# An RMSNorm with SiLU on one core: the root by GpSimd's power, squares moved to ScalarE, gamma in one piece, VectorE's instructions at an edge

## The chip, the core and the metric

The kernel runs on one core of a Trainium2 chip. The metric is device time in microseconds (us). Three runs before the change took 316.83, 316.88 and 316.90 us; their median is 316.88. One further execution was profiled. Its span, from the first to the last instruction, is 315.43 us.

## What is computed

```python
def reference(x, gamma, eps):
    rms = np.sqrt(np.mean(x ** 2, axis=-1, keepdims=True) + eps)
    out = gamma * x / rms
    return (out * (1 / (1 + np.exp(-out)))).astype(np.float32)
```

x has the shape 8 x 1024 x 2048 in float32, so 8192 rows of 2048 numbers; gamma has 2048 and eps is 1e-5. 67.1 MB are read and 67.1 MB written.

## The kernel before

The 8192 rows are cut into 16 blocks of 512. A block lies in SBUF as 128 partitions with J = 4 rows each, 32 KB a partition, 4.19 MB in all. A ring of BUFS = 6 such blocks (`xt`) holds the data; a block is loaded, worked on in place and stored from the same place. So load b + 6 has to wait until store b has landed. Blocks 4 and 5 are loaded by one transfer of twice the size (`load_pair`, L69).

Loads are issued from ScalarE's instruction stream (L67, L71), stores from SyncE's (L117). Each stream runs in its own order, so an instruction that waits holds what stands behind it. The order is written out by hand (`tc.manual_schedule`, L119).

A block b passes these steps:

- `squares_scalar(b)` (L73) and `squares_vector(b)` (L84): the sum of squares of each of its four rows. ScalarE does the first `share(b)` rows with Square and an accumulator (L78), VectorE the others with a multiply-and-reduce (L86). Each of these shows in the profile as two instructions, the operation and the reading of the accumulator. The results go to `ss`, 128 x 4. `share` is 2, but 1 for the even blocks from 4 to 12. The products themselves go to PSUM and are not used.
- `root(b)` (L93): ScalarE takes the square root of ss / d + eps (L95). In the trace a table load (ACT_TABLE_LOAD) precedes each change between Sqrt and Silu; Square has none of its own beside either.
- `invert(b)` (L98): VectorE's reciprocal of that, `rstd`, 128 x 4 (L100).
- `multiply(b)` (L103): VectorE multiplies each row by its rstd and by gamma, four instructions (L105), each with two tensors of SBUF as inputs.
- `silu(b)` (L108): ScalarE applies Silu to two rows at a time (L113), then SyncE issues the store. The argument `between` issues a load between the two halves.

The main loop (L145) does the squares and the root of block b + 1 together with the product and the Silu of block b: for the first three blocks and the last one the product comes first, for the others the squares. From block 8 on, the load of block b + 3 is issued within `squares_scalar(b + 1)`, behind its first square; loads 6 and 7 are issued at b = 3. The last block (L174) is done in another way: VectorE multiplies each row by gamma alone (L177) and ScalarE's Silu takes rstd as its scale, row by row (L179).

At the start gamma is loaded into one partition (L125), copied to all 128 by TensorE with a matrix of ones (L128) and brought from PSUM to `g` by VectorE (L130). A Square of one element (L124) warms ScalarE up. Lines 198 and 212 in the profile stand for the framework's instructions at the start and at the end.

The instructions of an engine are read from memory in blocks, by transfers of their own (queue q14 in the profile).

Of the kernel before, what the change touches and what calls it, by code (L numbers as in the profile page):

```python
# [1 line left out]

# [4 lines left out]

ACT = mybir.ActivationFunctionType
ALU = mybir.AluOpType


@with_exitstack
def kernel(
    ctx: ExitStack,
    tc: tile.TileContext,
    x: bass.AP,
    gamma: bass.AP,
    eps: bass.AP,
    out: bass.AP,
):  # L20

    nc = tc.nc
    P = nc.NUM_PARTITIONS
    f32 = mybir.dt.float32
    x2 = x.flatten_outer_dims()
    o2 = out.flatten_outer_dims()  # L30
    n, d = x2.shape
    J = 4
    BUFS = 6
    nblk = n // (P * J)
    PAIRS = (4,)

    def view(t, b):

        for q in PAIRS:
            if b in (q, q + 1):  # L40
                both = t[q * P * J:(q + 2) * P * J, :].rearrange("(p j) d -> p (j d)", p=P, j=2 * J)
                return both[:, (b - q) * J * d:(b - q + 1) * J * d]
        return t[b * P * J:(b + 1) * P * J, :].rearrange("(p j) d -> p (j d)", p=P, j=J)

    singles = ctx.enter_context(tc.tile_pool(name="singles", bufs=1))
    small = ctx.enter_context(tc.tile_pool(name="small", bufs=2))
    psum = ctx.enter_context(tc.tile_pool(name="psum", bufs=1, space=bass.MemoryType.PSUM))

    Q = 4
    w = d // Q  # L50
    g = singles.tile([P, d], f32)
    eps_t = singles.tile([P, 1], f32)
    ones = singles.tile([P, P], f32)
    junk_a = psum.tile([P, d], f32, name="junk_a")
    junk_v = psum.tile([P, d], f32, name="junk_v")
    ring = singles.tile([P, BUFS * J * d], f32, name="xt")
    sss, rmss, rstds = {}, {}, {}

    def rows(b, j, k):
        at = (b % BUFS) * J + j  # L60
        return ring[:, at * d:(at + k) * d]

    def row(b, j):
        return rows(b, j, 1)

    def load(b):
        nc.scalar.dma_start(out=rows(b, 0, J), in_=view(x2, b))  # L67

    def load_pair(b):  # L69
        both = x2[b * P * J:(b + 2) * P * J, :].rearrange("(p j) d -> p (j d)", p=P, j=2 * J)  # L70
        nc.scalar.dma_start(out=rows(b, 0, 2 * J), in_=both)  # L71

    def squares_scalar(b, loads=()):  # L73


        sss[b] = small.tile([P, J], f32, name="ss")
        for j in range(share(b)):
            nc.scalar.activation(out=junk_a, in_=row(b, j), func=ACT.Square,  # L78
                                 accum_out=sss[b][:, j:j + 1])
            if j == 0:  # L80
                for s in loads:
                    load(s)

    def squares_vector(b):  # L84
        for j in range(share(b), J):
            nc.vector.tensor_tensor_reduce(  # L86
                out=junk_v, in0=row(b, j), in1=row(b, j), scale=1.0, scalar=0.0,
                op0=ALU.mult, op1=ALU.add, accum_out=sss[b][:, j:j + 1])

    def share(b):  # L90
        return 1 if 4 <= b <= 12 and b % 2 == 0 else 2

    def root(b):  # L93
        rms = small.tile([P, J], f32, name="rms")
        nc.scalar.activation(out=rms, in_=sss.pop(b), func=ACT.Sqrt, scale=1.0 / d, bias=eps_t)  # L95
        rmss[b] = rms

    def invert(b):  # L98
        rstd = small.tile([P, J], f32, name="rstd")
        nc.vector.reciprocal(out=rstd, in_=rmss.pop(b))  # L100
        rstds[b] = rstd

    def multiply(b):  # L103
        for j in range(J):
            nc.vector.scalar_tensor_tensor(out=row(b, j), in0=row(b, j), scalar=rstds[b][:, j:j + 1],  # L105
                                           in1=g, op0=ALU.mult, op1=ALU.mult)

    def silu(b, between=()):  # L108
        for h in range(0, J, 2):
            if h:  # L110
                for s in between:
                    load(s)
            nc.scalar.activation(out=rows(b, h, 2), in_=rows(b, h, 2), func=ACT.Silu)  # L113
        store(b)

    def store(b):
        nc.sync.dma_start(out=view(o2, b), in_=rows(b, 0, J))  # L117

    with tc.manual_schedule():  # L119

        load(0)
        nc.vector.memset(ones, 1.0)  # L122
        nc.vector.memset(eps_t, float(eps))
        nc.scalar.activation(out=junk_a[:, 0:1], in_=ones[:, 0:1], func=ACT.Square)  # L124
        nc.sync.dma_start(out=g[0:1, :], in_=bass.AP(tensor=gamma.tensor, offset=gamma.offset, ap=[[d, 1], [1, d]]))  # L125
        for c in range(Q):
            cols = slice(c * w, (c + 1) * w)
            nc.tensor.matmul(junk_v[:, cols], ones[0:1, :], g[0:1, cols], start=True, stop=True)  # L128
        load(1)
        nc.vector.tensor_copy(out=g, in_=junk_v)  # L130
        nc.scalar.copy(out=junk_a[:, 0:1], in_=junk_v[:, d - 1:d])  # L131
        for b in range(2, PAIRS[0]):
            load(b)
        for b in PAIRS:
            load_pair(b)

        last = nblk - 1
        SOON = 3  # L140
        squares_scalar(0)
        squares_vector(0)
        root(0)
        invert(0)
        for b in range(last):  # L145
            loads = [b + 3] if BUFS + 2 <= b + 3 < nblk else []
            between = []
            if b + 3 == BUFS:

                load(BUFS)  # L150
                between = [BUFS + 1]
            if b < SOON:
                multiply(b)
                squares_scalar(b + 1, loads)
                silu(b)
                squares_vector(b + 1)
                root(b + 1)
            elif b < last - 1:
                squares_scalar(b + 1, loads)
                squares_vector(b + 1)  # L160
                root(b + 1)
                multiply(b)
                silu(b, between)
            else:
                multiply(b)
                squares_scalar(b + 1)
                silu(b)
                squares_vector(b + 1)
                root(b + 1)
            if b + 1 < last:  # L170
                invert(b + 1)


        for j in range(J):  # L174
            if j == J // 2:
                invert(last)
            nc.vector.tensor_mul(out=row(last, j), in0=row(last, j), in1=g)  # L177
        for j in range(J):
            nc.scalar.activation(out=row(last, j), in_=row(last, j), func=ACT.Silu,  # L179
                                 scale=rstds[last][:, j:j + 1])  # L180
        store(last)


# [1 line left out]
_INS = ['x', 'gamma', 'eps']  # L185
_OUTS = [((8, 1024, 2048), 'float32')]

_NUMBERS = {'eps': 9.999999747378752e-06}


# [26 lines left out]
```

## Time and profile before

| what | us |
|---|---|
| median of three runs | 316.88 |
| span of the profiled execution | 315.43 |
| VectorE (DVE) busy | 235.2 |
| ScalarE (ACT) busy | 212.5 |
| TensorE (PE) busy | 7.2 |
| GpSimd (POOL) busy | 0.2 |
| VectorE, 60 products (L105), 2.346 each | 137.0 |
| VectorE, 37 squares (L86), 2.296 each | 85.0 |
| ScalarE, 30 Silu of two rows (L113), 3.610 each | 107.3 |
| ScalarE, 27 squares (L78), 1.873 each | 50.6 |
| ScalarE, 31 table loads, 1.283 each | 39.8 |
| ScalarE, 16 square roots (L95), 0.297 each | 4.8 |
| first store issued, last store issued | 35.29, 291.55 |
| last store landed | 314.61 |

The table gives times of one execution, from the profiled one but for its first line. DMA stands for the 16 engines that move data between HBM and SBUF; all queues share them. A queue's transfer is made of packets; here most have 32 KB, one partition's four rows. The queue q10 holds the loads, q1 the stores and gamma. The profile's DMA line gives the busy share of the engines in tenths, in 40 equal slices of the span, and the packet records give the start, length, queue and size of each packet, without the engine that moved it. An idle time in the list of waits is put down to what ended it.

### The profile page before, as it was taken

Reading aid. Unit: us, or ns where it says so; the run is one execution under the profiler, and the core shown is the slowest. Engines: PE = TensorE matmul, PEld = TensorE weight load, DVE = VectorE, ACT = ScalarE, POOL = GpSimd, SP = SyncE. Lnnn points to the kernel's source line nnn. Section 1 sums busy time; section 2 is a strip of 40 time slices with the busy share of each in tenths; the row PEclk is TensorE's granted clock in tenths of the full one; section 3 lists DMA queues with packets and bytes.
Section 4 is the critical chain, followed back from the end, with each engine's and each line's share of the span. In section 5 each row is a group of like instructions: output and inputs, shape, how many; then the busy total and the mean of one; then the engine's idle time right before and its main releaser. Section 6 shows DMA issues by size and latency. Waiting matters only on the chain.

```text
span 315.4 us, 436 instructions
## 1 busy us (share of the span) xinstructions
PE 7.2 (2%) x8; PEld 2.5 (1%) x8; DVE 235.2 (75%) x157; ACT 212.5 (67%) x137; POOL 0.2 (0%) x4
## 2 busy tenths in 40 slices
PE   6300000000000000000000000000000000000000
PEld 2000000000000000000000000000000000000000
DVE  0679697944999999999693996939969399994000
ACT  1269998952289968993919849097591999999000
POOL 0000000000000000000000000000000000000000
DMA  8999999999999999999999999999999999999996
GB/s 333 411 453 411 386 532 399 399 440 424 428 437 424 437 432 432 432 432 440 424 440 424 445 420 457 407 457 407 465 399 465 399 465 399 465 403 461 411 453 270
DMA packets 4468, 134.24 MB, mean 426 GB/s; under 512 B 497, under 2 KB 497, under 8 KB 497
## 3 DMA queue, kind: packets, MB, share of 16 engines
q10 hardware_dynamic: 2160, 67.11, 49.6%
q1 hardware_dynamic: 2306, 67.12, 49.3%
q14 instruction: 2, 0.02, 0.0%
HBM read 67.12 MB, written 67.11 MB: 426 GB/s over the span
## 4 chain that ended last, share of the span: by engine, by line
DMA 55%; ACT 18%; DVE 14%; issue 2%; another core or an unknown queue 2%; ACTq 1%; DVEq 0%
DMA out_dram<-xt 40%; DMA xt<-in_x_dram 15%; ACT xt L113 9%; DVE xt L105 9%; DVE junk_v L86 5%; ACT junk_a L78 3%; ACT L95 2%; ACT xt L179 2%; ACT L113 1%; ACTq L212 1%; ACT rms L95 1%; ACTq L67 0%; ACT L179 0%; DVE rstd L100 0%
## 5 line engine op out<-in xcount | busy, mean ns | idle before, releaser
L105 DVE SCALAR_TENSOR_TENSOR xt<-xt,rstd,g 128x2048 f32<-128x2048 f32 x60 | 137.0, 2346 | 0.1
L113 ACT ACTIVATE xt<-xt 128x4096 f32<-128x4096 f32 x30 | 107.3, 3610 | 7.4 <-DVE xt L105 7.3
L86 DVE CUSTOM_DVE_ANT_0 junk_v<-xt 128x2048 f32<-128x2048 f32 x37 | 85.0, 2296 | 26.6 <-DMA xt<-in_x_dram 25.9
L78 ACT ACTIVATE junk_a<-xt 128x2048 f32<-128x2048 f32 x27 | 50.6, 1873 | 34.5 <-DMA out_dram<-xt 22.7
L95 ACT ACT_TABLE_LOAD x15 | 19.2, 1283 | 20.1 <-DMA out_dram<-xt 10.9
L113 ACT ACT_TABLE_LOAD x14 | 18.0, 1283 | 0.2
L100 DVE RECIPROCAL rstd<-rms 128x4 f32<-128x4 f32 x16 | 2.8, 174 | 15.0 <-ACT rms L95 15.0
L130 DVE COPY g<-junk_v 128x2048 f32<-128x2048 f32 x1 | 2.3, 2291 | 9.3 <-PE junk_v L128 9.3
L177 DVE TENSOR_TENSOR xt<-xt,g 128x2048 f32<-128x2048 f32 x4 | 8.9, 2278 | 0.0
L95 ACT ACTIVATE rms<-ss,eps_t 128x4 f32<-128x4 f32 x16 | 4.8, 297 | 5.5 <-DVE ss L86 5.3
L179 ACT ACTIVATE xt<-xt,rstd 128x2048 f32<-128x2048 f32 x4 | 7.7, 1990 | 0.0
L128 PE MATMUL junk_v<-g,ones 1*128 1x512 f32 x8 | 7.2, 1072 | 3.1 <-DMA g<-in_gamma_dram 3.1
L131 ACT COPY junk_a<-junk_v 128x1 f32<-128x1 f32 x1 | 0.1, 144 | 10.1 <-DVE g L130 10.1
L86 DVE DVE_READ_ACCUMULATOR2_ANT ss<- 128x1 f32 x37 | 5.2, 141 | 0.0
L78 ACT ACTIVATION_READ_ACCUMULATOR junk_a<-xt 128x1 f32 x27 | 5.0, 186 | 0.0
L128 PEld LDWEIGHTS junk_v<-g,ones 1*128 1x128 f32 x8 | 2.5, 325 | 6.2 <-issue 6.2
L124 ACT ACT_TABLE_LOAD x1 | 1.3, 1283 | 1.1 <-PEq L198 1.1
L179 ACT ACT_TABLE_LOAD x1 | 1.3, 1283 | 0.0
L122 DVE MEMSET ones<- 128x128 f32 x1 | 0.2, 165 | 0.8 <-PEq L198 0.8
L124 ACT ACTIVATE junk_a<-ones 128x1 f32<-128x1 f32 x1 | 0.2, 174 | 0.0
L198 POOL MEMSET const-bfloat16-1.0<- 128x1 bf16 x1 | 0.1, 103 | 0.0
L198 POOL MEMSET const-uint8-127<- 128x1 uint8 x1 | 0.1, 103 | 0.0
(3 smaller groups left out, 0.3 us busy)
## 6 DMA issues: line engine op xcount, KB each, us to landing
out_dram<-xt SPq DMA_DIRECT2D x16, 4096.0 KB, 39.1
xt<-in_x_dram ACTq DMA_DIRECT2D x14, 4096.0 KB, 26.6
g<-in_gamma_dram SPq DMA_DIRECT2D x1, 8.0 KB
xt<-in_x_dram ACTq DMA_DIRECT2D x1, 61.8
```

The source lines that it names most:

```text
L78: nc.scalar.activation(out=junk_a, in_=row(b, j), func=ACT.Square, accum_out=sss[b][:, j:j + 1])
L86: nc.vector.tensor_tensor_reduce(out=junk_v, in0=row(b, j), in1=row(b, j), scale=1.0, scalar=0.0, op0=ALU.mult, op1=ALU.add, accum_out=sss ...
L95: nc.scalar.activation(out=rms, in_=sss.pop(b), func=ACT.Sqrt, scale=1.0 / d, bias=eps_t)
L100: nc.vector.reciprocal(out=rstd, in_=rmss.pop(b))
L105: nc.vector.scalar_tensor_tensor(out=row(b, j), in0=row(b, j), scalar=rstds[b][:, j:j + 1], in1=g, op0=ALU.mult, op1=ALU.mult)
L113: nc.scalar.activation(out=rows(b, h, 2), in_=rows(b, h, 2), func=ACT.Silu)
L124: nc.scalar.activation(out=junk_a[:, 0:1], in_=ones[:, 0:1], func=ACT.Square)
L128: nc.tensor.matmul(junk_v[:, cols], ones[0:1, :], g[0:1, cols], start=True, stop=True)
L130: nc.vector.tensor_copy(out=g, in_=junk_v)
L177: nc.vector.tensor_mul(out=row(last, j), in0=row(last, j), in1=g)
L179: nc.scalar.activation(out=row(last, j), in_=row(last, j), func=ACT.Silu, scale=rstds[last][:, j:j + 1])
L212: with _tile.TileContext(nc) as tc:
```

## The change

The root leaves ScalarE and VectorE. `root(b)` now has two instructions on GpSimd: ss / d + eps, and that to the power -0.5, with the exponents in a small tile `expo` that GpSimd fills once. `invert` and `eps_t` are gone.

`share(b)` becomes 3 for the blocks 4 to 14, and stays 2 for 0 to 3 and for 15.

`plain(b)` holds for the blocks 5 to 10 and for 15. There VectorE multiplies all four rows by gamma in one instruction, without rstd, and Silu takes rstd as its scale, row by row, four instructions. The last block goes through the same functions as the others; its Silu starts when the whole product is there.

`addr_align(SLOTS, max_nops=0)` stands on VectorE ahead of its first instruction of the kernel. When the program is loaded, it puts the next instruction of that engine at a multiple of 128 instructions, and the engine jumps over the gap. From there on VectorE has 118 instructions.

```diff
+    SLOTS = 128
+    SOON = 3
...
-    eps_t = singles.tile([P, 1], f32)
+    expo = singles.tile([P, J], f32)
...
     def share(b):
-        return 1 if 4 <= b <= 12 and b % 2 == 0 else 2
+        return 3 if 4 <= b < nblk - 1 else 2
 
     def root(b):
-        rms = small.tile([P, J], f32, name="rms")
-        nc.scalar.activation(out=rms, in_=sss.pop(b), func=ACT.Sqrt, scale=1.0 / d, bias=eps_t)
-        rmss[b] = rms
-
-    def invert(b):
+        ms = small.tile([P, J], f32, name="ms")
         rstd = small.tile([P, J], f32, name="rstd")
-        nc.vector.reciprocal(out=rstd, in_=rmss.pop(b))
+        nc.gpsimd.tensor_scalar(out=ms, in0=sss.pop(b), scalar1=1.0 / d, scalar2=float(eps),
+                                op0=ALU.mult, op1=ALU.add)
+        nc.gpsimd.tensor_tensor(out=rstd, in0=ms, in1=expo, op=ALU.pow)
         rstds[b] = rstd
 
+    def plain(b):
+        return b == nblk - 1 or SOON + 2 <= b < SOON + 8
+
     def multiply(b):
+        if plain(b):
+            whole = rows(b, 0, J).rearrange("p (j d) -> p j d", j=J)
+            nc.vector.tensor_mul(out=whole, in0=whole, in1=g.unsqueeze(1).to_broadcast([P, J, d]))
+            return
         for j in range(J):
...
-            nc.scalar.activation(out=rows(b, h, 2), in_=rows(b, h, 2), func=ACT.Silu)
+            if plain(b):
+                for j in (h, h + 1):
+                    nc.scalar.activation(out=row(b, j), in_=row(b, j), func=ACT.Silu,
+                                         scale=rstds[b][:, j:j + 1])
+            else:
+                nc.scalar.activation(out=rows(b, h, 2), in_=rows(b, h, 2), func=ACT.Silu)
         store(b)
...
         load(0)
+        nc.vector.addr_align(SLOTS, max_nops=0)
         nc.vector.memset(ones, 1.0)
-        nc.vector.memset(eps_t, float(eps))
+        nc.gpsimd.memset(expo, -0.5)
...
         root(0)
-        invert(0)
...
-            if b + 1 < last:
-                invert(b + 1)
-
-
-        for j in range(J):
-            if j == J // 2:
-                invert(last)
-            nc.vector.tensor_mul(out=row(last, j), in0=row(last, j), in1=g)
-        for j in range(J):
-            nc.scalar.activation(out=row(last, j), in_=row(last, j), func=ACT.Silu,
-                                 scale=rstds[last][:, j:j + 1])
-        store(last)
+        multiply(last)
+        silu(last)
```

## The prediction

> **What bounds the kernel now.** I read the page first, then the waits of the store queue, then windows of DMA load, then the packet records themselves.
>
> ```profile
> span 315.4 us, 436 instructions
> PE 7.2 (2%) x8; PEld 2.5 (1%) x8; DVE 235.2 (75%) x157; ACT 212.5 (67%) x137; POOL 0.2 (0%) x4
> DMA  8999999999999999999999999999999999999996
> DMA packets 4468, 134.24 MB, mean 426 GB/s; under 512 B 497, under 2 KB 497, under 8 KB 497
> q14 instruction: 2, 0.02, 0.0%
> DMA out_dram<-xt 40%; DMA xt<-in_x_dram 15%; ACT xt L113 9%; DVE xt L105 9%; DVE junk_v L86 5%; ACT junk_a L78 3%; ACT L95 2%; ACT xt L179 2%; ACT L113 1%; ACTq L212 1%; ACT rms L95 1%; ACTq L67 0%; ACT L179 0%; DVE rstd L100 0%
> ```
>
> No compute engine is full, while the DMA line shows a 9 in all but the first and the last of 40 slices. The chain gives 55% to transfers. Two packets of q14 are instruction fetches; they matter below.
>
> The next view gives stretches: PE, PEld, DVE, ACT and POOL busy, the clock, the DMA share and GB/s.
>
> ```profile
> 40.00:270.00 230.00, 0.00 (x0) 0.00 (x0) 193.92 (x129) 166.75 (x105) 0.00 (x0) 1.00 1.00 433
> 270.00:312.00 42.00, 0.00 (x0) 0.00 (x0) 17.09 (x11) 21.44 (x13) 0.00 (x0) 1.00 1.00 431
> 35.00:40.00 5.00, 0.00 (x0) 0.00 (x0) 3.06 (x3) 4.94 (x6) 0.00 (x0) 1.00 1.11 419
> 313.00:314.00 1.00, 0.00 (x0) 0.00 (x0) 0.00 (x0) 0.00 (x0) 0.00 (x0) 1.00 0.08 33
> ```
>
> From 40 us on the 16 DMA engines are full at 433 GB/s. 134.24 MB / 433 GB/s is 310.0 us of the 315.43, so the whole change can win only from the other 5.4: the start (first packet at 1.64 us), a dip in 35 to 40 us (spread over packet times, 373 GB/s there: 5 x (1 - 373/433) = 0.69 us), and the end, where 33 GB/s means that hardly more than one engine of the 16 still works.
>
> The packet records say which. Each engine works back to back (a 32 KB packet takes 1.213 us), so matching each end with the next start strings the packets into 16 chains. Fourteen chains without a fetch end between 312.90 and 313.32 us. The chain with the fetch at 92.71 us ends at 313.39. The chain with the fetch at 106.49 us ends at **314.28**, 0.89 us after the second last. Around it: fetch 0.309 us, then a load packet of 1.747 instead of 1.213, so 0.309 + 0.534 = 0.84 us. At 92.71: fetch 0.309, then a store packet of 1.333, so 0.43 us. In both cases a load packet was in front and the store queue was next; at 106.49 its next packet was only the 4-byte end mark of store 2, so a load followed. The final transfer lands at 314.61, and 0.82 us of closing instructions make 315.43. The median, 316.88, is 1.45 us above this span; I keep that.
>
> **The compute edits cost nothing.** The slack is in the queues. Stores land every 19.35 us (127.14, 146.49, 165.83, 185.18 us), 8.4 MB at 433 GB/s. The store queue's waits:
>
> ```profile
> SPq L117 <- ACT xt L113: 262.0, 15, 29.3
> SPq L212 <- DMA out_dram<-xt: 22.5, 3, 9.6
> ```
>
> The first line is the queue waiting for work while earlier stores still flow. In the second, its last three entries wait 22.5 us for stores already issued: store 15 is issued at 291.55 and store 14 lands only at 304.96.
>
> Squares: ScalarE gets 43 (2 x 4 + 3 x 11 + 2) instead of 27, VectorE 21 instead of 37. ScalarE pays 16 x (1.873 + 0.186) = 32.9 us; VectorE saves 16 x (2.296 + 0.141) = 39.0.
>
> Sqrt and its tables: 16 x 0.297 = 4.8 us and about 29 of 31 table loads x 1.283 = 37 us leave ScalarE (the warm-up and the first Silu may keep one each); 16 reciprocals of 0.174 leave VectorE.
>
> Scaling moved into Silu: the four L179 instructions take 7.68 us against 7.12 for an L113 pair, so 6 x 0.56 = +3.4 us on ScalarE. The one-piece product is not in the trace: between 4 x (2.278 - 0.165) = 8.45 (0.165, the 128x128 memset, as fixed part) and 4 x 2.278 = 9.11 us; I take 8.7, against 9.14 for the four L105. Last block: the Silu now waits for the whole product (product from 278.2 to about 287, four Silu 7.7: store 15 near 295 instead of 291.6), still 10 us before 305.
>
> Per block that is 3 x 2.04 + 7.1 to 7.7 = at most 13.8 us on ScalarE and 2.4 + 9.14 = 11.5 on VectorE, inside 19.35.
>
> GpSimd root: two dependent instructions of 128x4 replace a chain of 1.28 + 0.30 + 0.17 = 1.75 us. GpSimd's only row is a memset of 0.103 us, so from below 2 x 0.1; from above I take the longest elementwise row, 2 x 2.35 = 4.7. I choose 2 us, nearer the small tiles (0.17 to 0.30). Behind the power wait the four products of its block on VectorE and, through them, Silu and store. At the last block rstd is needed by 293 (8 us of Silu, store out by 301), and the sums are ready at 278.3: cover of 15 us. All blocks earlier are covered by a store queue that is one to two blocks deep.
>
> First store: 35.29 us now, set by products, then Silu, so the same within 3 us; loads alone fill the engines until past 60 us. The added memset of expo is off every path, eps_t's is gone.
>
> **The fetches are the only term.** Fetches are of 8192 B. That one holds 128 instructions, the edge of the change, fits what the trace shows: streams of 175 records (VectorE) and 177 (ScalarE), two fetches in all, so one crossing each. (The Trainium skill, Vector Engine (DVE) Microarchitecture Reference, Instruction fetch and dispatch, gives 64 B an instruction, so 128.) ScalarE starts its 59th record at 91.69 and VectorE its 62nd at 105.38, each about 1.0 us ahead of a fetch packet, the same delay as from load 0's issue (0.73) to its first packet (1.74). So I give 92.71 to ScalarE and 106.49 to VectorE (the other way round, 69th and 52nd, fits less evenly). With 118 instructions from an edge on, VectorE crosses none while data move. Its jump to the edge comes at about 0.8 us; a fetch of the following block would come near 1.7, where the engines start unevenly anyway (first packets 1.64 to 2.88), and the engine that carried gamma's 1.045 us packet there ended at 313.32, not late.
>
> ScalarE keeps its crossing: 177 records + 32 - 29 - 16 + 12 = 176, so one crossing, not two. Its 60th record falls in the squares of block 6, right behind load 8, which waits for store 2 (107.85). The fetch comes then at 109 to 111, with store 3 in full flow: 0.43 us. On a chain that would end at 312.90 to 313.32 this gives 313.33 to 313.75; I take 313.5. Against 314.28 that is **-0.78 us**: span 314.65, time 316.1. If VectorE's jump stalls for its block, ones is late by some 2 us; PE waits for gamma until 3.0 anyway, and loads 0 and 1 (8.4 MB, 19 us) cover it.
>
> The Trainium skill (Runtime: NRT & Kernel Launch, Instruction fetch mechanics) says fetches come in blocks of 256 instructions and that the cost of crossing is mostly hidden. Here packets hold 128, and one crossing stands open at the end of the trace with 0.89 us; by that rule the change would give 316.9, the second rival.
>
> **Rivals.**
> 1. *Another fetch meets an exposed load.* ScalarE's crossing slips ahead of load 8's wait, beside store 2's end (106.4), or GpSimd crosses too: its 16 records become 65 to 80, and a 60th would come past 200 us. With 0.84 us on a chain: 313.74 to 314.16, time 316.3 to 316.8. For it: one fetch of two did so. Against: with both queues full the store follows the fetch.
> 2. *The edit does not do what it says*, or the late chain was late for another reason: 316.9. Against: 1.747 stands directly behind the fetch.
> 3. *The dip at 35 to 40 us goes too.* It comes with the first store (issued 35.29, first packet about 39.3). If it needs an empty store queue it stays; if a shifted first store avoids it, another 0.69: 315.4.
> 4. *Slower: the root is held on GpSimd.* Place: root(15), between 278.3 and the Silu. From 15 us for the pair the end moves one for one; a root of 20 us gives 316.1 + 5 = 321. Every square and product on VectorE reads two SBUF tensors back to back, and a one-piece product lasts 8.7; if each of the two instructions waited for one to pass, 17.4 + 2 = 19.4 us, about 320.5. Against: the last such product starts with root(15) and only one can stand in the way. The Trainium skill (GPSIMD Engine Reference, Key points) states such contention between GpSimd and VectorE instructions with two SBUF inputs; no run here shows it.
>
> **How the numbers follow.** The forecast has 0.58, rival 1 0.18, rival 2 0.08, rival 3 0.06, rival 4 with any other slowing 0.10. A measurement of this kernel tells about 0.2% from no change, 0.63 us, so faster means below 316.25. Of the forecast's 315.9 to 316.35 I put 0.48 below that and 0.10 above. Faster: 0.48 + 0.06 = 0.54. Within 0.2%: 0.10 + 0.18 + 0.08 = 0.36. Slower: 0.10. The range 315.75 to 316.95 holds the forecast and rivals 1 and 2, 0.84, and leaves out rivals 3 and 4.
>
> **What would show it.** Right: one or two q14 packets in the span, none of them VectorE's; from 313.0 on under 70 GB/s only for some 0.5 us; last landing near 313.8; 433 GB/s from 40 to 270 us unchanged; store 15 issued before 301. The steps on compute are wrong if the DMA line shows a slice below 9 between 40 us and the end, or if the store queue waits for Silu after 305. The term is wrong if the last packets still end at 314.2 with VectorE's fetch gone, or if a chain with no fetch ends last.

## The result, and the profile after

The changed kernel takes 317.54 us (median of 21 runs, 317.06 to 317.93); the kernel before, run beside it, 316.92 (21 runs). The ratio is 1.0017 with a 95% interval of 1.001 to 1.0023: a loss of 0.2% where a gain of 0.8 us was forecast, and outside the range that ended at 316.95.

The profiled execution of the kernel after belongs to a run of 317.13 us. Its page:

```profile
span 315.0 us, 436 instructions
PE 7.2 (2%) x8; PEld 2.5 (1%) x8; DVE 192.9 (61%) x87; ACT 204.7 (65%) x136; POOL 40.6 (13%) x37
DMA  8999999999999999999999999999999999999996
DMA packets 4468, 134.24 MB, mean 426 GB/s; under 512 B 497, under 2 KB 497, under 8 KB 497
q14 instruction: 2, 0.02, 0.0%
DMA out_dram<-xt 53%; DVE xt L112 9%; ACT xt L122 6%; ACT junk_a L80 5%; DMA xt<-in_x_dram 4%; ACT xt L125 4%; POOL ms L98 3%; DVE junk_v L88 3%; POOL rstd L100 1%; ACTq L215 1%; ACTq L69 0%; POOLq L215 0%; DVE ss L88 0%; POOLq L98 0%; DVEq L88 0%
```

VectorE is busy for 42 us less, ScalarE for 8 less, and the transfers are as before. The same stretches as before the change, DMA share and GB/s in the last two columns:

```profile
40.00:270.00 230.00, 0.00 (x0) 0.00 (x0) 152.08 (x66) 164.42 (x109) 28.24 (x26) 1.00 1.00 433
270.00:312.00 42.00, 0.00 (x0) 0.00 (x0) 15.17 (x6) 18.22 (x10) 9.69 (x2) 1.00 1.01 435
35.00:40.00 5.00, 0.00 (x0) 0.00 (x0) 4.76 (x3) 4.83 (x6) 0.21 (x1) 1.00 1.09 413
313.00:314.00 1.00, 0.00 (x0) 0.00 (x0) 0.00 (x0) 0.00 (x0) 0.00 (x0) 1.00 0.01 0
```

433 GB/s again from 40 to 270 us, the dip at 35 to 40 is still there, and hardly a packet starts behind 313. The store queue:

```profile
SPq L129 <- ACT xt L125: 152.4, 9, 29.2
SPq L129 <- ACT xt L122: 89.6, 7, 14.0
SPq L215 <- DMA out_dram<-xt: 19.3, 2, 9.6
```

Its last two entries still wait 19.3 us for stores already issued, so the compute is covered at the end, as forecast.

**Where the loss is.** The span of this profile is 0.42 us shorter than the one before the change (315.01 against 315.43). But a run's time is its span and something around it. For the kernel after the rest is 2.11 us (2.07 to 2.16 in 21 runs). For the kernel before the spans of the 21 runs beside it are not on record; in the three groups of 33, 31 and 9 later runs that have them the rest is 1.78 to 1.81. I had taken 1.45 from two different executions, the profiled one and the median, and had assumed that the change leaves it alone. The first loss, 0.32 us, is thus outside the span. The median spans are 315.4 after and 315.1 to 315.2 before, so the other part of the loss, 0.2 to 0.3 us, is inside.

The packet records, strung into 16 chains as before, show the fetches. Two views of q14, in 3.5 to 4.5 us and in 316 to 317 us, the first within the load-only start, the second behind the span's end:

```profile
q14 instruction: 1, 0.01, 1.9%
...
q14 instruction: 1, 0.01, 3.1%
```

So VectorE's fetch did not vanish. It left 106 us, and one came at 3.76 us, behind its jump. ScalarE's is at 112.1 us, 1 us behind the place that was expected, with a store packet next and 0.42 us lost. The one at 316.48 us is new.

### The profile page after: what moved, and what is told of

Read it like the earlier page. It is cut to its first block, busy times and chain, and to the rows that moved or that the text cites. A ratio compares the mean times of both kernels' runs of the same rounds, so it can differ in the third digit from the quotient of the medians.

```text
span 315.0 us, 436 instructions
## 1 busy us (share of the span) xinstructions
PE 7.2 (2%) x8; PEld 2.5 (1%) x8; DVE 192.9 (61%) x87; ACT 204.7 (65%) x136; POOL 40.6 (13%) x37
## 4 chain that ended last, share of the span: by engine, by line
DMA 57%; ACT 14%; DVE 12%; issue 5%; POOL 4%; ACTq 1%; POOLq 0%; DVEq 0%
DMA out_dram<-xt 53%; DVE xt L112 9%; ACT xt L122 6%; ACT junk_a L80 5%; DMA xt<-in_x_dram 4%; ACT xt L125 4%; POOL ms L98 3%; DVE junk_v L88 3%; POOL rstd L100 1%; ACTq L215 1%; ACTq L69 0%; POOLq L215 0%; DVE ss L88 0%; POOLq L98 0%; DVEq L88 0%
## 5 line engine op out<-in xcount | busy, mean ns | idle before, releaser
L80 ACT ACTIVATE junk_a<-xt 128x2048 f32<-128x2048 f32 x43 | 80.6, 1875 | 63.6 <-DMA out_dram<-xt 42.5
L88 DVE CUSTOM_DVE_ANT_0 junk_v<-xt 128x2048 f32<-128x2048 f32 x21 | 48.3, 2298 | 76.6 <-DMA xt<-in_x_dram 76.5
L112 DVE SCALAR_TENSOR_TENSOR xt<-xt,rstd,g 128x2048 f32<-128x2048 f32 x36 | 82.2, 2347 | 5.7 <-POOL rstd L100 5.7
L125 ACT ACTIVATE xt<-xt 128x4096 f32<-128x4096 f32 x18 | 64.4, 3607 | 8.9 <-DVE xt L112 5.8
L109 DVE TENSOR_TENSOR xt<-xt,g 128x8192 f32<-128x8192 f32 x7 | 60.8, 8688 | 0.1
L122 ACT ACTIVATE xt<-xt,rstd 128x2048 f32<-128x2048 f32 x28 | 53.7, 1987 | 5.9 <-POOL rstd L100 5.9
L98 POOL TENSOR_SCALAR ms<-ss 128x4 f32<-128x4 f32 x16 | 13.9, 869 | 244.0 <-ACT junk_a L80 170.2
L100 POOL TENSOR_TENSOR rstd<-ms,expo 128x4 f32<-128x4 f32 x16 | 26.4, 1653 | 1.3
L80 ACT ACTIVATION_READ_ACCUMULATOR junk_a<-xt 128x1 f32 x43 | 8.0, 186 | 0.0
L88 DVE DVE_READ_ACCUMULATOR2_ANT ss<- 128x1 f32 x21 | 3.0, 141 | 0.0
```

What stands on the lines that cost most here:

```text
L88: nc.vector.tensor_tensor_reduce(out=junk_v, in0=row(b, j), in1=row(b, j), scale=1.0, scalar=0.0, op0=ALU.mult, op1=ALU.add, accum_out=sss ...
L98: nc.gpsimd.tensor_scalar(out=ms, in0=sss.pop(b), scalar1=1.0 / d, scalar2=float(eps), op0=ALU.mult, op1=ALU.add)
L100: nc.gpsimd.tensor_tensor(out=rstd, in0=ms, in1=expo, op=ALU.pow)
L109: nc.vector.tensor_mul(out=whole, in0=whole, in1=g.unsqueeze(1).to_broadcast([P, J, d]))
L122: nc.scalar.activation(out=row(b, j), in_=row(b, j), func=ACT.Silu, scale=rstds[b][:, j:j + 1])
```

## The experiments

Each kernel ran beside the kernel before on one chip. "Outside" is a run's time less its span, as a median; GpSimd's records count all rows of its stream in the trace, waits too.

| kernel | GpSimd records | VectorE's first slot | median us | outside | span |
|---|---|---|---|---|---|
| before | 16 | as it falls | 316.92 to 316.99 | 1.78 to 1.81 | 315.1 to 315.2 |
| after | 67 | 0 | 317.54 | 2.11 | 315.4 |
| e1, after without the edge | 67 | as it falls | 317.20 | 2.12 | 315.1 |
| e2, after with Sqrt | 16 | 0 | 317.56 | 2.20 | 315.4 |
| e3, e2 without the edge | 16 | as it falls | 316.82 | 1.80 | 315.0 |
| e4, before with GpSimd's root | 67 | as it falls | 317.09 | 2.13 | 315.0 |
| e5, e2 at slot 100 | 16 | 100 | 317.40 | 1.77 | 315.6 |
| e6, e2 at slot 64 | 16 | 64 | 317.59 | 1.79 | 315.8 |
| e7, e3 with one idle power | 20 | as it falls | 316.94 | 1.77 | 315.2 |
| e8, e3 with 51 memsets | 67 | as it falls | 317.19 | 2.10 | 315.1 |
| e9, e1 with the sum scaled on VectorE | 44 | as it falls | 346.69 | 1.79 | 344.9 |

**Power and edge apart.** e1 takes the edge out of the kernel after, e2 the power, e3 both; e4 puts the power alone into the kernel before.

```diff
e1
-        nc.vector.addr_align(SLOTS, max_nops=0)
e2: in the kernel after (e3: the same and without addr_align)
     def root(b):
...
-        nc.gpsimd.tensor_scalar(out=ms, in0=sss.pop(b), scalar1=1.0 / d, scalar2=float(eps),
-                                op0=ALU.mult, op1=ALU.add)
-        nc.gpsimd.tensor_tensor(out=rstd, in0=ms, in1=expo, op=ALU.pow)
+        nc.scalar.activation(out=rms, in_=sss.pop(b), func=ACT.Sqrt, scale=1.0 / d, bias=eps_t)
+        rmss[b] = rms
+    def invert(b):
+        rstd = small.tile([P, J], f32, name="rstd")
+        nc.vector.reciprocal(out=rstd, in_=rmss.pop(b))
+        rstds[b] = rstd
e4: the reverse of this in the kernel before
```

> The kernel after, without the jump to an edge. Theory G (GpSimd's power and its two configuration instructions cost the 0.66 us that the kernel after has outside its span, 2.11 against 1.45): still 2.1 us outside. Theory A (the jump moves VectorE's closing instructions across another edge, and the fetch seen 1.5 us behind the span costs it): 1.45 outside. For the span, theory F (the jump's fetch at 3.76 us met the load-only stretch and made the late chain, and its wait behind a first load packet makes the spans scatter from 314.9 to 315.8): no instruction packet before 90 us, VectorE's back in the mixed stretch at 0.43 us, last packet at 313.3 to 313.75, spans near 314.6 with a scatter under 0.2. Rival to F: the scatter comes from GpSimd or the new order, and spans stay between 314.9 and 315.8.

> The kernel after with the root of before (Sqrt on ScalarE, reciprocal on VectorE), the jump kept. Theory G: 1.45 us outside the span. Theory A: 2.1. Theory F: an instruction packet near 3.8 us again, a chain that ends near 313.8 or later, spans between 314.9 and 315.8, so 316.4 to 317.2 in all by G. VectorE has some 134 instructions here, so one more fetch may come near the end of the run.

> The kernel after with the root of before and without the jump: three squares on ScalarE and the one-piece product alone. G and F together: 1.45 us outside, two instruction packets between 85 and 130 us, span near 314.6 if both are followed by a store packet (0.43 us each), so 316.1; 316.9 if one is followed by a load. If the early compute, not the fetch, made the spans scatter: 316.4 to 317.2.

> The kernel before with GpSimd's root alone. Theory G: 2.1 us outside the span, so about 317.5 where the span is 315.4 as before, 316.7 if the moved fetches both meet a store. Theory A: 1.45 outside.

Ratios to the kernel before: e1 1.0007 (0.9998 to 1.0015), e2 1.002 (1.001 to 1.0029), e3 0.9998 (0.9989 to 1.0007), e4 1.0001 (0.9992 to 1.0009). Outside the span, G and A were both half right: the power alone gives 2.12 and 2.13, the edge alone 2.20, both together no more than one, 2.11. All three kernels with GpSimd's root have an instruction packet 1.4 to 1.5 us behind the span; e2 and e3 have none.

Within the span, e2 against e3 and the kernel after against e1 give the edge +0.4 and +0.3 us (only the first two ran side by side). The compute edits without the edge (e3) move the span by -0.2 and the time by nothing that can be told. The spans near 314.6 that were expected of e1 and e3 did not come: they are 315.1 (314.8 to 315.4) and 315.0 (314.9 to 315.4). VectorE's crossing cost its DMA engine 0.66 us there and not 0.43, and e3 has a third packet, at 249.4 us.

**Number of instructions, or the power?** e7 and e8 add instructions on GpSimd to e3, whose results nothing uses; e5 and e6 move the edge in e2.

```diff
e5, e6 (64)
-        nc.vector.addr_align(SLOTS, max_nops=0)
+        nc.vector.addr_align(SLOTS, offset=100, max_nops=0)
e7
+        nc.gpsimd.memset(spare, 2.0)
+        nc.gpsimd.tensor_tensor(out=spare2, in0=spare, in1=spare, op=ALU.pow)
e8
+        for _ in range(51):
+            nc.gpsimd.memset(spare, 2.0)
```

> The third kernel of before this (root by Sqrt, no jump; 1.80 us outside the span, span 315.0) with a short jump: VectorE's first instruction at slot 100 of 128 instead of 0. If VectorE starts near slot 66 naturally, as its crossing at the 62nd record says, the jump stays in its block. Theory F (the early fetch comes from entering a new block): no instruction packet at 3.7 us, crossing near the 28th instruction, 40 to 50 us, span near 315.0. Theory C (the time outside grows when an engine's closing instructions cross an edge): the last of some 126 stands at slot 226, the closing crosses or not as it did before, 1.80 outside, 316.8 in all. Rival J (any jump costs it): 2.2 outside, 317.2 or more.

> The same with slot 64, which lies behind the natural start by less than a block, so the jump enters the next block in its middle. F: an instruction packet near 3.7 us again, a further one when VectorE crosses at its 64th instruction, span near 315.4. C: the last instruction near slot 190, the closing crosses nothing, 1.80 outside, 317.2 in all. J: 2.2 outside, 317.6.

> Root by Sqrt, no jump, and one idle power of a 128x4 tile on GpSimd at the start, whose result nothing uses. Theory G (GpSimd's power and its configuration cost the time outside): 2.1 outside, 317.1 in all. Theory C (it is the number of GpSimd's instructions, 67 records, which makes its closing instructions cross an edge): 1.80 outside, 316.8, and no instruction packet behind the span.

> Root by Sqrt, no jump, and 51 memsets of a 128x4 tile on GpSimd at the start, no power, so that GpSimd has 67 records as with the power. C: an instruction packet 1.5 us behind the span and 2.1 outside, 317.1 in all. G: 1.80 outside, 316.8.

Outside the span, theory C holds on all four; the times of e5 and e6 are 0.6 and 0.4 us above what it said, because their spans are longer. The page of e8, the memsets in it, and its q14 in 316 to 317 us:

```profile
PE 7.2 (2%) x8; PEld 2.5 (1%) x8; DVE 195.6 (62%) x104; ACT 247.6 (79%) x181; POOL 5.4 (2%) x55
L139 POOL MEMSET spare<- 128x4 f32 x51 | 5.2, 101 | 3.2 <-POOLq L209 0.3
...
q14 instruction: 1, 0.01, 3.4%
```

51 memsets of 0.101 us, done within the first 10 us, where GpSimd is otherwise idle, cost 0.30 us outside the span (2.10 against 1.80), with an instruction packet at 316.5 us, behind the span's end. The power itself costs nothing there (e7: 1.77). On VectorE slot 0 costs 0.4 us outside (2.20), slots 64 and 100 nothing, with the same instructions. For GpSimd the packet shows the crossing; in e2 none is recorded behind the span, so for VectorE it is inferred from the slot alone.

F holds for where the early packet comes from, in part. With slot 64 there is one at 3.92 us and another at 138.5 (65 records behind the jump), and both fall on one engine: it ends at 314.60, the median engine at 313.09, and the median span, 315.8 (315.7 to 316.2), is the longest of e1 to e8. With slot 100 none comes at the jump, but one at 23.6 us, earlier than the 40 to 50 expected; I did not find out why. It met the load-only stretch and cost its engine 0.92 us (next packet 1.799). Two profiles of e5 (the second is e12) show spans of 315.2 and 315.1 with that engine last (314.03 and 313.99), while its runs reach 316.5; those long ones no profile caught.

**A version meant to win.** e9 is e1 with the first of GpSimd's two instructions moved to VectorE, so that GpSimd keeps 44 records.

```diff
-        nc.gpsimd.tensor_scalar(out=ms, in0=sss.pop(b), scalar1=1.0 / d, scalar2=float(eps),
+        nc.vector.tensor_scalar(out=ms, in0=sss.pop(b), scalar1=1.0 / d, scalar2=float(eps),
```

> The kernel after without the jump, and with ss / d + eps moved from GpSimd to VectorE, so that only the power is left on GpSimd: some 50 records there instead of 67. Theory C: its closing instructions cross no edge, no packet behind the span, 1.79 us outside instead of 2.12, span as in the kernel without the jump (315.1), 316.9 in all. Theory G: 2.1 outside, 317.2.

Outside, 1.79 as C said, and no packet behind the span. But the span is 344.9 us, 30 more. The waits of its VectorE and ScalarE, in us in total, times, longest:

```profile
DVE ms L98 <- ACT junk_a L80: 102.6, 11, 11.6
ACT xt L122 <- DVE xt L109: 53.6, 6, 8.9
ACT xt L125 <- DVE xt L112: 33.4, 13, 4.8
```

And one block in order of time, start, length and engine:

```profile
225.90 1.86 ACT L80 ACTIVATE junk_a<-xt 128x2048 f32<-128x2048 f32 x1
...
231.76 0.19 ACT L80 ACTIVATION_READ_ACCUMULATOR junk_a<-xt 128x1 f32 x1
232.04 0.17 DVE L98 TENSOR_SCALAR ms<-ss 128x4 f32<-128x4 f32 x1 [11.55 <-ACT junk_a L80]
232.12 8.69 DVE L109 TENSOR_TENSOR xt<-xt,g 128x8192 f32<-128x8192 f32 x1
232.29 9.38 POOL L100 TENSOR_TENSOR rstd<-ms,expo 128x4 f32<-128x4 f32 x1 [13.20 <-DVE ms L98]
...
240.89 2.00 ACT L122 ACTIVATE xt<-xt,rstd 128x2048 f32<-128x2048 f32 x1 [8.95 <-DVE xt L109]
```

The product of block b stands in VectorE's order behind `ms` of block b + 1, and that waits for ScalarE's third square. ScalarE's Silu of block b then waits for the product, and its next squares stand behind the Silu. So three squares (6.1), a product (8.7 or 9.1) and the Silu (7.1 to 7.7) run one behind the other: 22.6 us from one `ms` to the next (232.04 to 254.62), over the 19.35 that the transfers need. The queues, which the forecast counted as cover, ran dry: the DMA share falls to 0.92 (368 GB/s) in 235 to 258 us. In the kernel after GpSimd takes this wait, and nothing stands behind it there but the next root:

```profile
235.00:258.00 23.00, 0.00 (x0) 0.00 (x0) 11.45 (x6) 13.57 (x10) 9.70 (x2) 1.00 0.92 368
...
POOL ms L98 <- ACT junk_a L80: 170.2, 11, 18.1
```

The first line is of e9, the second of the kernel after. That is the real worth of its root.

**Which engine ends last.** Seven more profiles, six of the kernel after and one of e5 (e12), unchanged.

> The kernel after, unchanged, for another profile: its spans lay between 314.9 and 315.8 and the one profile so far at 314.96. Theory F: the engine that carries the fetch near 3.7 us ends last, and a longer span means that this engine ends later, up to 314.6. Rival: all engines end later together, which would be a common loss in the load-only stretch or at the first store.

> The kernel after once more, unchanged. F: the engine with the fetch near 3.7 us ends last by itself, later by as much as the span is longer. Rival: all 16 engines end later together.

> The short jump to slot 100 once more, whose spans lay between 314.9 and 316.5 with one profile at 315.2: F says that the engine with the fetch near 23.6 us ends last by itself, up to 315.7; the rival that all 16 end later together.

> The kernel after, unchanged, for its profile. If the span is over 315.3: theory F has the engine of the packet near 3.7 us end last, 0.8 us or more behind the median engine; theory D (the dip at the first store, which strikes single engines harder when the engines are out of step) has an engine without such a packet end last, with 1.3 us or more lost between 33 and 46 us against 0.7 in the median.

> The same kernel and the same two readings: by F the engine of the early packet ends last in a long span, by D another one that lost 1.3 us or more at the first store.

> The same kernel and the same two readings: by F the engine of the early packet ends last in a long span, by D another one that lost 1.3 us or more at the first store.

> The same kernel and the same two readings: by F the engine of the early packet ends last in a long span, by D another one that lost 1.3 us or more at the first store.

With the first one there are seven profiles of the kernel after, in order of their spans:

| span | last engine ends | what it carried | median engine |
|---|---|---|---|
| 314.8 | 313.63 | the early packet (3.69) | 313.22 |
| 314.8 | 313.64 | the early packet (3.69) | 313.26 |
| 315.0 | 313.84, and 313.80 | no early packet, 0.4 late at 5 us, 0.80 lost at the first store, 0.19 at 55 us; and the early packet (3.76) | 313.16 |
| 315.1 | 313.94 | ScalarE's packet (112.6) | 313.16 |
| 315.2 | 314.08 | the early packet (3.83) | 313.31 |
| 315.3 | 314.15 | no early packet, 1.88 lost at the first store | 313.29 |
| 315.3 | 314.09 | no early packet, 1.93 lost at the first store | 313.37 |

F and D both occur. The prediction had named a chain with no fetch that ends last as a sign that its term is wrong, and three of the seven show one. An engine's lateness is its time less 1.21 us for each load or store packet done. The engine of the early packet is 0.7 us late at 5 us (3.31 to 3.51 against 2.61 to 2.68 in the median), gets part of it back at the first store, where it loses 0.3 to 0.8 instead of the usual 0.7 to 0.9, and ends 0.35 to 0.8 behind the median. In the two longest spans another engine lost 1.9 us between 33 and 46 us. No profile fell on a span of 315.4 to 315.8, which 13 of the first 21 runs had, so what makes those stays open.

## Why the prediction was wrong, by its steps

**"The median, 316.88, is 1.45 us above this span; I keep that."** This step failed, for 0.32 us of the loss. Taken run by run the rest is 1.8 us before, and the change makes it 2.11, because GpSimd's stream grows from 16 to 67 records (e8 shows it with memsets alone) and VectorE's starts at slot 0 (e2; e5 and e6 take it away by the slot alone); either suffices. The prediction counted 65 to 80 records for GpSimd and priced a crossing within the span; it came behind it, where no transfer hides it.

**"Against 314.28 that is -0.78 us."** This step failed by more: the span moved by +0.2 to +0.3 and not by -0.78, so that the sign would have been missed with the rest unchanged too. A single late engine of one execution was taken as the kernel's usual end. Of 74 recorded spans of before 72 lie between 315.0 and 315.6, with a median of 315.2; the profiled 315.43 was a long one, so about 0.2 us of the gain was not there to be had. Nor was the crossing all that made that engine late: it was 0.34 us behind the median at 5 us already (3.01 against 2.67), 100 us ahead of its fetch.

**"VectorE crosses none while data move", and a fetch near 1.7 us costs nothing.** The crossing at 106 us went, as said, but entering the new block brought a fetch. It waited behind its engine's first load packet (1.824 + 1.935 = 3.76 us) and then cost 0.307 and a load packet of 1.749 instead of 1.213. That engine ended 0.35 to 0.8 us behind the median, about what a crossing in the mixed stretch costs (e1 to e8: 0.66 us for VectorE, 0.42 to 0.52 for ScalarE). The edge moved the cost and did not remove it. One profile does not fit: in e2 the early packet (3.71 us) had a load packet of 1.213 behind it and cost 0.30, its engine ended at the median (313.28), and the engine of ScalarE's two packets ended last (314.05); so what the edge costs within e2's span stays open. No kernel here runs without a fetch by VectorE while data move, so the gain of its absence was not measured. The likeness to the engine of gamma's packet was wrong: that packet comes ahead of the first load, this one behind it.

**ScalarE's crossing** at 109 to 111 us with 0.43 us: right in size (0.42) and near in place (112.1, in the other profiles of the kernel after up to 114.8).

**The compute edits cost nothing**: right, but with a condition that the prediction did not see: here the longest wait, up to 18.1 us, is GpSimd's, with nothing else behind it; on VectorE the same join costs 30 us (e9). The one-piece product took 8.688 us (8.7 taken), the last store left before 295, and VectorE's and ScalarE's busy times fell as summed.

**GpSimd's root** was put at 2 us; unhindered it takes 0.194 + 1.007 = 1.2. Rival 4's mechanism is real. The last product and root(15) ran together:

```profile
276.62 8.69 DVE L109 TENSOR_TENSOR xt<-xt,g 128x8192 f32<-128x8192 f32 x1
276.67 8.69 POOL L98 TENSOR_SCALAR ms<-ss 128x4 f32<-128x4 f32 x1 [14.00 <-DVE ss L88]
280.60 13.92 SPq L129 DMA_DIRECT2D out_dram<-xt  x2
285.44 1.01 POOL L100 TENSOR_TENSOR rstd<-ms,expo 128x4 f32<-128x4 f32 x1
```

GpSimd's first instruction lasted exactly as long as VectorE's product; only one stood in the way, the pair took 9.8 us, under the 15 that were covered, and the last store left at 294.2. So its price here is nothing, as argued. The Trainium skill (GPSIMD Engine Reference, Key points) states this contention, and the trace agrees: 8.687 us beside a product, 0.194 else.

**Rival 2** (hidden, 316.9) came nearest to the time, for another reason: fetches are not hidden, but the change only moves them. The Trainium skill (Runtime: NRT & Kernel Launch, Instruction fetch mechanics) calls the crossing mostly hidden; here it costs its DMA engine 0.30 to 0.92 us and, in the closing instructions, 0.3 us of the run.

## What to carry to other kernels

Where the transfers fill the span, compare runs by span and rest, each from the same run, before a profile's tail is read as a gain: the rest can change too, and one late engine of one execution is a sample. An edge for instructions moves a fetch and adds one where it is entered; count the instructions of idle engines as well, since their closing code can cross an edge behind the last transfer. A join of two engines belongs on an engine with nothing queued behind the wait.

## What the runs showed of the hardware that was not expected

- An instruction packet of 8192 B costs its DMA engine more than its own 0.31 us in all but one place (e2's early one, 0.30): 0.42 in all for ScalarE's with a store packet next (1.326 to 1.334; 0.52 with 1.427 in e2 and e6), 0.66 for VectorE's in the mixed stretch (next packet 1.56), 0.84 when a load follows the end mark of a store, 0.84 to 0.92 in the load-only stretch.
- Packets of one engine's stream fall on one chain: in e6 both of VectorE's, in e2, e3 and e5 to e8 both of ScalarE's (92.7 to 95.1 and about 250 us, where Sqrt raises its records to 221). Their costs add up.
- GpSimd's small instructions were held by VectorE's instruction with two SBUF inputs beside them: the power that began at 100.87 us, 0.2 us behind a product of 8.69, ended 0.86 us behind the product's end, and the power took between 1.006 and 9.341 us:

```profile
L98 POOL TENSOR_SCALAR ms<-ss x16: 193/194/8687, 18.6 to 276.7; 128x4 f32<-128x4 f32 x16
L100 POOL TENSOR_TENSOR rstd<-ms,expo x16: 1006/1007/9341, 18.9 to 285.4; 128x4 f32<-128x4 f32 x16
```

- At the first store the DMA engines lose time once (33 to 46 us): the median engine 0.6 to 0.9 us, single ones between 0.3 and 1.9. All profiles show it, and no kernel here avoided it.
